# The mixers' output products of a decoder trunk: o stationary, 512 columns of weights moving, and turned back to features

## The chip, the cores and the metric

The kernel runs on one core of one Trainium2 chip. The time is that of the device in microseconds (us), the median of several runs. "Span" is the time from the first to the last instruction in one execution that the hardware profiler took.

## The reference

A trunk of two layers over 256 tokens of width 1024, in float32. Each layer is a half-weighted SwiGLU feed-forward (width 2816), a mixer with attention (16 heads of 64), and a second feed-forward; each has an RMSNorm ahead of it.

```python
for layer in range(DEPTH):
    h = h + 0.5 * swiglu(rmsnorm(h, ffn1_norm[layer]), ...)
    hn = rmsnorm(h, mix_norm[layer])
    h = h + (mixer_a(hn, ...) if layer == 0 else mixer_b(hn, ..., shared))
    h = h + 0.5 * swiglu(rmsnorm(h, ffn2_norm[layer]), ...)
    if layer == 0:
        shared = shared_kv(h, kv_norm, kv_w, pos)
return rmsnorm(h, final_norm)
```

Both mixers end in `o @ w_o`, where o is the attention's output (256 tokens by 1024) and w_o is 1024 by 1024. Mixer a takes q, k and v from one projection of the stream; mixer b takes q from its own norm of the stream and k, v from a second norm, the shared one. At this length mixer b's attention is plain causal attention, and mixer a's three dilated patterns become one mask with the logarithm of counts.

## The kernel before, in words

**Layout.** The stream is kept with features on the partitions: hT is 8 blocks of 128 features by 256 tokens. A norm (class Norm, L219) has three parts. `scale` (L231) writes a block of x = h times the gain, as a high part on ScalarE and a low part on VectorE (L98, L96); products are made as three, high by high, high by low, low by high, so that float32 is kept. `square` (L234) squares a block on ScalarE and adds it on GpSimd into ss (L237, L240, L241). `finish` (L243) lets TensorE sum ss over the partitions (L246: a column of one number for each token), VectorE add epsilon (L248: v_n) and GpSimd take the power -0.5 (L250: c_n). The norm's factor is applied after the product, at the evacuation.

**Weights** come in pieces: a DMA on the queue of SyncE into raw, ScalarE's copy wh (the high part), VectorE's difference wl (the low part). A piece of 128 by 1024 is one place of 8 in the pool wp; the class Pieces (L292) splits a few pieces ahead of their use. The feed-forward's first pieces (f20_g0, f20_u0, f20_g2 and so on, L166, L167) are split during the mixer's last part, some of them behind given instructions of the attention (`queued`, L145).

**Mixers** (L722) run products and attention interleaved on TensorE by a hand-written agenda (L266). The generator `projections` (L789) makes products of a segment of 512 columns of weights for two tiles of 128 tokens and says what each step of three matmuls costs (0.68). Calls due by the agenda's clock run in between: `norm.late` (the turning back that the feed-forward ahead has left over), `norm.finish` at 8.1 if the norm's column isn't there, and the attention's steps. `evacuate` (L767) takes a finished accumulator: ScalarE scales it by the column (rt, L772), VectorE rotates (L635 to L638), and `turn_in` (L752) is put on the agenda, which transposes q and k on TensorE (L761: qt) at 4.4 - 1.2t after the evacuation of the first segment. Then come scores (s), transposes of the weights of attention (pt, L682), their parts pT (L684, L687), products with v (po, L701, L703), and a block of the output, oT, with features on the partitions (L705, L710, L98, L94). There are 8 blocks; the last one also loads ScalarE's table for Silu (L718).

**Output products** (`out_t`, L591). For each block k of o, 4 accumulators of 2 blocks of output features by 256 tokens take 6 matmuls each: the weights are stationary (128 by 128) and o moves (256 columns). The pieces of the last three blocks are held until all of o is there; then each accumulator is finished in turn, VectorE adds it to hT (L622), the next norm scales the blocks, and after all of them the norm squares. The feed-forward (`ffn_blocks`, L351) follows, block k = 0 first, so it needs x of block 0 first.

**Down projections** (`down`, L542) already work the other way: tokens on the partitions, 512 columns of weights moving. Their results are turned back by 8 transposes for each pair of quarters (`turn`, L547 to L557), the second pair after the next stage has begun (`norm.late`).

Order: the Tile framework's scheduler sets each engine's order from the order of the program and its own estimates, so that an instruction's place in a queue can change when the program around it does.

Of the kernel before, what the change touches and what calls it, by code (L numbers as in the profile page):

```python
# [66 lines left out]
def trunk(ctx: ExitStack, tc: tile.TileContext, a: dict, out: bass.AP):  # L67
    nc = tc.nc
# [15 lines left out]
    def acc(name):  # L84
        return accp.tile([P, 512], F32, tag="acc", name=name)
# [18 lines left out]
    def trt(name):  # L104
        return trp.tile([P, 512], F32, tag="tr", name=name)
# [83 lines left out]
    def product(accs, xh, xl, ws, first, last):  # L189

        for ac, (wh, wl) in zip(accs, ws):
            nc.tensor.matmul(ac, xh, wh, start=first, stop=False)  # L192
        for ac, (wh, wl) in zip(accs, ws):
            nc.tensor.matmul(ac, xh, wl, start=False, stop=False)  # L194
        for ac, (wh, wl) in zip(accs, ws):
            nc.tensor.matmul(ac, xl, wh, start=False, stop=last)  # L196
# [252 lines left out]
    def quartered(name, w, acts, sums, weight, collected, tail=2):  # L449
# [89 lines left out]

        return close  # L540

    def down(name, w, acts, sums, norm):  # L542

        outs = []
        close = quartered(name, w, acts, sums, 0.5, outs.extend)

        def turn(c, half):  # L547
            tr = trt(f"dt_{name}_{c}_{half}")
            for i in range(2):
                for t in range(NT):  # L550
                    at = i * S + t * P
                    nc.tensor.transpose(tr[:, at:at + P], outs[t][c][:, (2 * half + i) * P:(2 * half + i + 1) * P], ident)
            d = 4 * c + 2 * half
            h = hT[:, d:d + 2, :]
            nc.vector.tensor_add(h, tr.rearrange("p (k s) -> p k s", s=S), h)
            for i in range(2):
                norm.block(d + i)  # L557

        def turn_first():
            for half in range(2):  # L560
                turn(0, half)

        for c in range(2):
            for t in range(NT):
                ac = close(t, c, between=turn_first if (t, c) == (0, 1) else None)
                nc.vector.scalar_tensor_tensor(outs[t][c], ac, 0.5, outs[t][c], op0=ALU.mult, op1=ALU.add)
        norm.late += [lambda half=half: turn(1, half) for half in range(2)]

    def down_last(name, w, acts, sums, h, weight, part, after):

# [20 lines left out]
    def out_t(name, pieces, base, blocks, norm, queue, tail=3):  # L591


        accs = [acc(f"ot_{name}_{i}") for i in range(KD // 2)]

        def step(i, k, ws):
            wh, wl = ws
            for j in range(2):
                d = slice((2 * i + j) * P, (2 * i + j + 1) * P)
                ac = accs[i][:, j * S:(j + 1) * S]  # L600
                hi, lo = blocks[k][:, 0, :], blocks[k][:, 1, :]
                nc.tensor.matmul(ac, wh[:, d], hi, start=k == 0 and j == 0, stop=False)
                nc.tensor.matmul(ac, wh[:, d], lo, start=False, stop=False)
                nc.tensor.matmul(ac, wl[:, d], hi, start=False, stop=k == KD - 1 and j == 1)

        for k in range(KD - tail):
            with queued(queue.get(k)):
                ws = pieces.get(base + k, 3)[0]
            while len(blocks) <= k:
                yield None  # L610
            for i in range(KD // 2):
                step(i, k, ws)
                yield 0.72
        held = [(k, pieces[base + k][0]) for k in range(KD - tail, KD)]
        while len(blocks) < KD:
            yield None
        for i in range(KD // 2):
            for k, ws in held:
                step(i, k, ws)
            for j in range(2):  # L620
                d = 2 * i + j
                nc.vector.tensor_add(hT[:, d, :], accs[i][:, j * S:(j + 1) * S], hT[:, d, :])  # L622
                norm.scale(d)
        for d in range(KD):
            norm.square(d)


    def rotate(v, t, name):
# [93 lines left out]
    def mixer(name, segs, plan, wo, mask, after, queue={}):  # L722

        n = HG * DH
        blocks, heads, qks, vss = [], {}, {}, {}
        specs = []
        for i, (norm, x, parts) in enumerate(segs):  # L730
            ends = [0]
            for part in parts:
                ends.append(ends[-1] + part[3])
            for k0 in range(0, KD, 4):
                specs.append((f"{''.join(part[0] for part in parts)}{name}{i}_{k0}", 4, ends[-1],
                              [(slice(at, at + c), rows(w, k0, 4, c0, c)) for at, (_, w, c0, c, _) in zip(ends, parts)]))
        base = 2 * len(specs)
        specs += [(f"{name}o_{u}", 2, D, [(None, rows(wo, 2 * u, 2, 0, D))]) for u in range(KD // 2)]
        pieces = Pieces(specs)
        agenda = Agenda()  # L740
        for norm in {id(norm): norm for norm, _, _ in segs}.values():
            for i in range(len(norm.late)):
                agenda.after(1.5 + 0.5 * i, lambda norm=norm: norm.late.pop(0)())
            if norm.col is None:
                agenda.after(8.1, norm.finish)
        scores, turn, values = attention(agenda, lambda g: (qks[g], vss.get(g)), mask, name, blocks)

        def turns(p):
            for i in range(2):
                turn(p, i)  # L750

        def turn_in(g, t):  # L752

            if t == 0:
                qks[g] = [ap_.tile([P, 4, NT, P], F32R, tag=f"qk{i}", name=f"qk{i}_{name}{g}", bufs=2) for i in "hl"]
            tr = trt(f"qt_{name}{g}_{t}")
            for i, kind in enumerate("qk"):
                s = heads[kind, g, t].rearrange("p a b -> p (a b)")
                for k in range(2):
                    at = (2 * i + k) * P  # L760
                    nc.tensor.transpose(tr[:, at:at + P], s[:, k * P:(k + 1) * P], ident)  # L761
            parts_of(*[x[:, :, t, :] for x in qks[g]], tr.rearrange("p (k n) -> p k n", n=P), later=agenda.soon)
            if t == NT - 1:
                for wait, step, p in plan[g]:
                    agenda.after(wait, {"s": scores, "t": turns, "v": values}[step], p)

        def evacuate(i, t, r, ac, parts):  # L767
            at, turned = 0, []
            wide = sum(c for kind, _, _, c, _ in parts if kind != "v")
            if wide:  # L770
                rt = atile([P, wide // DH, DH], name=f"rt_{name}{i}_{t}")
                nc.scalar.activation(flat(rt), ac[:, :wide], AF.Copy, scale=r)  # L772
# [12 lines left out]
            for g in sorted(set(turned)):  # L785
                if ("q", g, t) in heads and ("k", g, t) in heads:
                    agenda.after(4.4 - 1.2 * t if i == 0 else 3.2, turn_in, g, t)

        def projections():  # L789
            for i, (norm, x, parts) in enumerate(segs):  # L790
                acs = [acc(f"{''.join(part[0] for part in parts)}_{name}{i}_{t}") for t in range(NT)]
                for k0 in range(0, KD, 4):
                    for t in range(NT):
                        for k in range(k0, k0 + 4):
                            w = pieces[4 * i + k // 2][k % 2]
                            product([acs[t]], *x[t](k), [w], k == 0, k == KD - 1)
                            yield 0.68
                        if k0 + 4 == KD:
                            evacuate(i, t, norm.col[t], acs[t], parts)

        agenda.run(projections())
        agenda.run(out_t(f"{name}o", pieces, base, blocks, after, queue))
# [121 lines left out]
```

## Time and profile before

| | |
|---|---|
| median of 3 runs | 980.07 us (979.99 to 980.25) |
| the profiled execution | 980.13 us, span 978.4 |
| granted TensorE clock | 0.998 |
| mixer a, its output products | 277.8 to 307.8 us |
| mixer b, its output products | 758.2 to 789.35 us |
| TensorE busy in these two stretches | 29.73 of 30.00, 31.02 of 31.15 us |
| DMA over the span | 176.00 MB, 180 GB/s |

The page gives the busy time of each engine (PE is TensorE's matmuls, PEld its weight loads, DVE VectorE, ACT ScalarE, POOL GpSimd), and the chain of work that ended last. A row of the timeline has the start in us, the duration, the engine, the line, the operation, output<-inputs and the shape; idle time just before it stands in brackets, with what ended it. Matmuls overlap, so their cost is read from start to start. A row of the chain has the start, the time that the chain spent there, and what it was.

### The profile page before, as it was taken

Reading aid. Unit: us, or ns where it says so; the run is one execution under the profiler, and the core shown is the slowest. Engines: PE = TensorE matmul, PEld = TensorE weight load, DVE = VectorE, ACT = ScalarE, POOL = GpSimd, SP = SyncE. Lnnn points to the kernel's source line nnn. Section 1 sums busy time; section 2 is a strip of 40 time slices with the busy share of each in tenths; the row PEclk is TensorE's granted clock in tenths of the full one; section 3 lists DMA queues with packets and bytes.
Section 4 is the critical chain, followed back from the end, with each engine's and each line's share of the span. In section 5 each row is a group of like instructions: output and inputs, shape, how many; then the busy total and the mean of one; then the engine's idle time right before and its main releaser. Section 6 shows DMA issues by size and latency. Waiting matters only on the chain.

```text
span 978.4 us, 14860 instructions
## 1 busy us (share of the span) xinstructions
PE 967.5 (99%) x5391; PEld 831.9 (85%) x5391; DVE 813.0 (83%) x1383; ACT 612.7 (63%) x1131; POOL 287.0 (29%) x242
## 2 busy tenths in 40 slices
PE   8999999999999999999999999999999999999997
PEld 6888888878889888888888888888888998888886
DVE  7988899887878788889898888987787878888995
ACT  7655657567777665556576655655677756666561
POOL 3211246132332211146032121612142322112461
PEclk9999999999999999999999999999999999999999
DMA  9875536664334556546755556483734345564341
GB/s 317 259 238 187 197 133 216 219 212 157 133 98 152 180 186 189 184 153 208 256 172 173 172 177 212 169 277 114 249 131 136 116 145 172 186 202 173 130 172 43
DMA packets 126857, 176.00 MB, mean 180 GB/s; under 512 B 3392, under 2 KB 106304, under 8 KB 126784
## 3 DMA queue, kind: packets, MB, share of 16 engines
q1 hardware_dynamic: 125936, 174.01, 53.7%
q10 hardware_dynamic: 848, 1.05, 0.3%
q8 instruction: 42, 0.69, 0.3%
q14 instruction: 31, 0.25, 0.1%
HBM read 173.99 MB, written 1.05 MB: 179 GB/s over the span
## 4 chain that ended last, share of the span: by engine, by line
PE 92%; DVE 4%; ACT 2%; issue 1%; POOL 1%; DMA 0%; SPq 0%; POOLq 0%; DVEq 0%; ACTq 0%
PE f_g L203 16%; PE f_u L203 16%; PE f_u L206 8%; PE f_g L206 8%; PE dn_f_d L196 6%; PE dn_f_d L192 6%; PE dn_f_d L194 6%; PE dn_f_d_m L196 1%; PE dn_f_d_m L194 1%; PE dn_f_d_m L192 1%; PE qk_a L192 1%; PE qk_a L196 1%; PE qk_a L194 1%; DVE x_n L96 1%; PE q_b L192 1%
## 5 line engine op out<-in xcount | busy, mean ns | idle before, releaser
L368 POOL TENSOR_TENSOR j_f_u<-j_f_u,r_n 128x256 f32<-128x256 f32 x88 | 92.3, 1051 | 360.8 <-DVE j_f_u L336 338.0
L203 PE MATMUL f_g<-x_n,wh_f_g 128*128 128x512 f32 x688 | 180.5, 394 | 0.0
L203 PE MATMUL f_u<-x_n,wh_f_u 128*128 128x512 f32 x688 | 177.2, 390 | 0.0
L203 PEld LDWEIGHTS f_u<-x_n,wh_f_u 128*128 128x128 f32 x688 | 129.2, 188 | 27.3
L203 PEld LDWEIGHTS f_g<-x_n,wh_f_g 128*128 128x128 f32 x688 | 124.0, 189 | 22.7
L167 DVE TENSOR_TENSOR wl_f_u<-raw_f_u,wh_f_u 128x1024 fp32r<-128x1024 f32 x86 | 113.1, 1316 | 1.1 <-ACT wh_f_u L166 1.0
L167 DVE TENSOR_TENSOR wl_f_g<-raw_f_g,wh_f_g 128x1024 fp32r<-128x1024 f32 x86 | 104.3, 1230 | 2.8 <-ACT wh_f_g L166 2.8
L206 PE MATMUL f_u<-x_n,wl_f_u 128*128 128x256 f32 x688 | 103.3, 283 | 0.0
L206 PE MATMUL f_g<-x_n,wl_f_g 128*128 128x256 f32 x688 | 102.7, 282 | 0.0
L206 PEld LDWEIGHTS f_g<-x_n,wl_f_g 128*128 128x128 f32 x688 | 96.4, 190 | 6.3
L166 ACT ACTIVATE wh_f_u<-raw_f_u 128x1024 fp32r<-128x1024 f32 x86 | 88.0, 1049 | 12.0 <-PE f_g L203 7.5
L166 ACT ACTIVATE wh_f_g<-raw_f_g 128x1024 fp32r<-128x1024 f32 x86 | 89.6, 1049 | 4.7 <-PE f_g L203 2.8
L206 PEld LDWEIGHTS f_u<-x_n,wl_f_u 128*128 128x128 f32 x688 | 91.6, 192 | 0.0
L366 ACT ACTIVATE j_f_g<-j_f_g 128x256 f32<-128x256 f32 x88 | 36.7, 417 | 87.2 <-DVE j_f_g L365 86.9
L241 POOL TENSOR_TENSOR ss_n<-ss_n,sq_n 128x256 f32<-128x256 f32 x42 | 38.4, 913 | 148.8 <-ACT sq_n L240 146.8
L98 ACT ACTIVATE act_f<-j_f_g 128x256 fp32r<-128x256 f32 x58 | 23.9, 418 | 56.4 <-DVE j_f_g L376 56.4
L376 DVE TENSOR_TENSOR j_f_g<-j_f_g,j_f_u 128x256 f32<-128x256 f32 x58 | 27.9, 487 | 30.1 <-POOL j_f_u L368 30.1
L484 POOL TENSOR_TENSOR sum_f_d_6b<-sum_f_d_6ac,raw_f_d 128x512 f32<-128x512 f32 x4 | 45.5, 11371 | 17.6 <-DVE sum_f_d_6ac L483 13.2
L336 DVE TENSOR_TENSOR j_f_g<-f_g,j_f_g 128x256 f32<-128x256 f32 x88 | 36.6, 416 | 11.9 <-ACT j_f_g L335 11.9
L677 POOL TENSOR_SCALAR sm_b<-sm_b,ls_b 128x128 f32<-128x128 f32 (+1 forms) x32 | 28.5, 907 | 55.7 <-DVE ls_b L675 29.6
L335 ACT ACTIVATE j_f_u<-f_u 128x256 f32<-128x256 f32 x88 | 33.0, 375 | 15.0 <-PE row_n L258 14.0
L365 DVE TENSOR_TENSOR j_f_g<-j_f_g,r_n 128x256 f32<-128x256 f32 x88 | 41.4, 474 | 0.7
(565 smaller groups left out, 2369.3 us busy)
## 6 DMA issues: line engine op xcount, KB each, us to landing
raw_f_d<-in_ffn_w_down_dram SPq DMA_DIRECT2D x44, 1024.0 KB, 4.9
raw_f_g<-in_ffn_w_gate_dram SPq DMA_DIRECT2D x43, 1024.0 KB, 5.2
raw_f_u<-in_ffn_w_up_dram SPq DMA_DIRECT2D x43, 1024.0 KB, 5.2
raw_qka<-in_a_w_qkv_dram SPq DMA_DIRECT2D x16, 512.0 KB, 4.7
raw_va<-in_a_w_qkv_dram SPq DMA_DIRECT2D x4, 1024.0 KB, 5.4
raw_ao<-in_a_w_o_dram SPq DMA_DIRECT2D x4, 1024.0 KB, 4.9
raw_kvb<-in_kv_w_dram SPq DMA_DIRECT2D x8, 512.0 KB, 4.7
raw_qb<-in_b_w_q_dram SPq DMA_DIRECT2D x4, 1024.0 KB, 5.9
```

The source lines that it names most:

```text
L166: nc.scalar.activation(wh, r, AF.Copy)
L167: nc.vector.tensor_sub(wl, r, wh.bitcast(F32))
L192: nc.tensor.matmul(ac, xh, wh, start=first, stop=False)
L194: nc.tensor.matmul(ac, xh, wl, start=False, stop=False)
L196: nc.tensor.matmul(ac, xl, wh, start=False, stop=last)
L203: nc.tensor.matmul(ac, wh, flat(x), start=first and i == 0, stop=False)
L206: nc.tensor.matmul(ac[:, :S], wl, x[:, 0, :], start=False, stop=last and i == len(ws) - 1)
L241: nc.gpsimd.tensor_tensor(self.ss, self.ss, sq, op=ALU.add)
L365: nc.vector.tensor_mul(g, g, norm.row)
L366: nc.scalar.activation(g, g, AF.Silu)
L368: nc.gpsimd.tensor_tensor(u, u, norm.row, op=ALU.mult)
L484: nc.gpsimd.tensor_tensor(b[:, 0], ac[:, 0], raw[:, 3], op=ALU.add)
```

## The change

`out_t` now has the accumulators of a down projection: two tiles of tokens by two halves of 512 output features. A block of o is stationary (128 by 128 of it) and 512 columns of weights move, so that a block k takes 4 steps of three matmuls. At the end the quarters of the first half are finished for both token tiles, then those of the second half; ScalarE copies each quarter to SBUF, and the quarters are turned back to features by the function of the down projections, now shared (`turn_back`): the first half ahead of the last held block of quarter (0, 1), the second half by `norm.late` after the feed-forward's first block. The norm squares each block right behind its scaling.

In the mixers `norm.finish` is due at 8.7 for the first segment's norm and at 14.0 for another one (in mixer b: n5). An evacuation is put on the agenda rather than done at once, 0.6 later if the column isn't there yet. The second `turn_in` of the first segment is due 0.4 later.

```diff
     def out_t(name, pieces, base, blocks, norm, queue, tail=3):
-        accs = [acc(f"ot_{name}_{i}") for i in range(KD // 2)]
-        def step(i, k, ws):
-            wh, wl = ws
-            for j in range(2):
-                d = slice((2 * i + j) * P, (2 * i + j + 1) * P)
-                ac = accs[i][:, j * S:(j + 1) * S]
-                hi, lo = blocks[k][:, 0, :], blocks[k][:, 1, :]
-                nc.tensor.matmul(ac, wh[:, d], hi, start=k == 0 and j == 0, stop=False)
-                nc.tensor.matmul(ac, wh[:, d], lo, start=False, stop=False)
-                nc.tensor.matmul(ac, wl[:, d], hi, start=False, stop=k == KD - 1 and j == 1)
+        accs = [[acc(f"ot_{name}_{t}{c}") for c in range(2)] for t in range(NT)]
+        outs = [[None, None] for t in range(NT)]
+        def step(t, c, k, w):
+            x = tuple(blocks[k][:, i, t * P:(t + 1) * P] for i in range(2))
+            product([accs[t][c]], *x, [tuple(v[:, c * 512:(c + 1) * 512] for v in w)], k == 0, k == KD - 1)
...
-        for i in range(KD // 2):
-            for k, ws in held:
-                step(i, k, ws)
-            for j in range(2):
-                d = 2 * i + j
-                nc.vector.tensor_add(hT[:, d, :], accs[i][:, j * S:(j + 1) * S], hT[:, d, :])
-                norm.scale(d)
-        for d in range(KD):
-            norm.square(d)
+        for c in range(2):
+            for t in range(NT):
+                for k, w in held:
+                    step(t, c, k, w)
+                    if (t, c, k) == (0, 1, KD - 2):
+                        for half in range(2):
+                            turn_back(name, outs, 0, half, norm)
+                outs[t][c] = atile([P, 512], name=f"out_{name}_{t}{c}")
+                nc.scalar.activation(outs[t][c], accs[t][c], AF.Copy)
+        norm.late += [lambda half=half: turn_back(name, outs, 1, half, norm) for half in range(2)]
...
-                agenda.after(8.1, norm.finish)
+                agenda.after(8.7 if norm is segs[0][0] else 14.0, norm.finish)
...
-                    agenda.after(4.4 - 1.2 * t if i == 0 else 3.2, turn_in, g, t)
+                    agenda.after(4.4 - 0.8 * t if i == 0 else 3.2, turn_in, g, t)
...
-                            evacuate(i, t, norm.col[t], acs[t], parts)
+                            agenda.after(0.6 if norm.col is None else 0.0,
+                                         lambda t=t, i=i, norm=norm, ac=acs[t], parts=parts:
+                                         evacuate(i, t, norm.col[t], ac, parts))
```

More of the change, by code (lines that the diff above doesn't have):

```diff
@@ L540, in quartered, with turn_back @@
         return close
+    def turn_back(name, outs, c, half, norm):
+        tr = trt(f"dt_{name}_{c}_{half}")
+        for i in range(2):
+            for t in range(NT):
+                at = i * S + t * P
+                nc.tensor.transpose(tr[:, at:at + P], outs[t][c][:, (2 * half + i) * P:(2 * half + i + 1) * P], ident)
+        d = 4 * c + 2 * half
+        h = hT[:, d:d + 2, :]
+        nc.vector.tensor_add(h, tr.rearrange("p (k s) -> p k s", s=S), h)
+        for i in range(2):
+            norm.block(d + i)
     def down(name, w, acts, sums, norm):
@@ L545, in down @@
         close = quartered(name, w, acts, sums, 0.5, outs.extend)
[L547 to L557, printed above, removed]
         def turn_first():
             for half in range(2):
-                turn(0, half)
+                turn_back(name, outs, 0, half, norm)
         for c in range(2):
@@ L566, in down @@
                 nc.vector.scalar_tensor_tensor(outs[t][c], ac, 0.5, outs[t][c], op0=ALU.mult, op1=ALU.add)
-        norm.late += [lambda half=half: turn(1, half) for half in range(2)]
+        norm.late += [lambda half=half: turn_back(name, outs, 1, half, norm) for half in range(2)]
     def down_last(name, w, acts, sums, h, weight, part, after):
@@ L591, in out_t @@
     def out_t(name, pieces, base, blocks, norm, queue, tail=3):
-        accs = [acc(f"ot_{name}_{i}") for i in range(KD // 2)]
-        def step(i, k, ws):
-            wh, wl = ws
-            for j in range(2):
-                d = slice((2 * i + j) * P, (2 * i + j + 1) * P)
-                ac = accs[i][:, j * S:(j + 1) * S]
-                hi, lo = blocks[k][:, 0, :], blocks[k][:, 1, :]
-                nc.tensor.matmul(ac, wh[:, d], hi, start=k == 0 and j == 0, stop=False)
-                nc.tensor.matmul(ac, wh[:, d], lo, start=False, stop=False)
-                nc.tensor.matmul(ac, wl[:, d], hi, start=False, stop=k == KD - 1 and j == 1)
+        accs = [[acc(f"ot_{name}_{t}{c}") for c in range(2)] for t in range(NT)]
[3 more added lines that the diff above has]
+            product([accs[t][c]], *x, [tuple(v[:, c * 512:(c + 1) * 512] for v in w)], k == 0, k == KD - 1)
         for k in range(KD - tail):
             with queued(queue.get(k)):
-                ws = pieces.get(base + k, 3)[0]
+                w = pieces.get(base + k, 3)[0]
             while len(blocks) <= k:
                 yield None
-            for i in range(KD // 2):
-                step(i, k, ws)
-                yield 0.72
+            for t in range(NT):
+                for c in range(2):
+                    step(t, c, k, w)
+                    yield 0.68
         held = [(k, pieces[base + k][0]) for k in range(KD - tail, KD)]
@@ L616, in out_t @@
             yield None
-        for i in range(KD // 2):
-            for k, ws in held:
-                step(i, k, ws)
-            for j in range(2):
-                d = 2 * i + j
-                nc.vector.tensor_add(hT[:, d, :], accs[i][:, j * S:(j + 1) * S], hT[:, d, :])
-                norm.scale(d)
-        for d in range(KD):
-            norm.square(d)
+        for c in range(2):
+            for t in range(NT):
+                for k, w in held:
+                    step(t, c, k, w)
+                    if (t, c, k) == (0, 1, KD - 2):
+                        for half in range(2):
+                            turn_back(name, outs, 0, half, norm)
+                outs[t][c] = atile([P, 512], name=f"out_{name}_{t}{c}")
+                nc.scalar.activation(outs[t][c], accs[t][c], AF.Copy)
+        norm.late += [lambda half=half: turn_back(name, outs, 1, half, norm) for half in range(2)]
     def rotate(v, t, name):
```

## The prediction

> **What bounds the kernel now.** I read the page first: the busy shares, then the chain that ended last.
>
> ```profile
> PE 967.5 (99%) x5391; PEld 831.9 (85%) x5391; DVE 813.0 (83%) x1383; ACT 612.7 (63%) x1131; POOL 287.0 (29%) x242
> PE 92%; DVE 4%; ACT 2%; issue 1%; POOL 1%; DMA 0%; SPq 0%; POOLq 0%; DVEq 0%; ACTq 0%
> ```
>
> TensorE is busy nearly all the time and carries 92% of the chain. So two things count in the mixers: how long TensorE's own work takes there, start to start, and where it stands still. I went through the starts of its matmuls in the timeline and noted each place where the next one started late. An engine beside it counts only through such a place.
>
> **TensorE's work in the output products.** In the timeline of PE the steps from start to start are even.
>
> ```profile
> 299.17 0.28 PE L602 MATMUL ot_ao<-oT_a,wh_ao 128*128 128x256 f32 x1
> 307.81 0.40 PE L203 MATMUL f_g<-x_n,wh_f_g 128*128 128x512 f32 x1
> 187.51 0.39 PE L192 MATMUL dn_f_d<-wh_f_d_9a,act_f 128*128 128x512 f32 x1
> 190.23 0.39 PE L192 MATMUL qk_a<-wh_qka,x_n 128*128 128x512 f32 x1
> 185.94 0.27 PE L552 MATMUL dt_f_d<-ident,co_f_d_a 128*128 128x128 f32 x1
> 187.04 0.40 PE L194 MATMUL dn_f_d<-wl_f_d_10b,act_f 128*128 128x512 f32 x1
> ```
>
> The held tail of mixer a is 3 pieces x 4 accumulators x 6 = 72 matmuls of 256 columns, from 299.17 to 307.81: 0.120 us each. The 12 matmuls of 512 columns from 187.51 to 190.23 take 0.2267 each (the new form: activations stationary, weights moving). A mixer has 8 blocks; each costs 24 x 0.120 = 2.88 before and 12 x 0.2267 = 2.72 after. That is 23.04 against 21.76, **-1.28 per mixer, -2.56 in all**.
>
> The Trainium skill (TensorE: Matmul & The Clock Gate, Back-to-back issue gap) gives a warm matmul N/2.4 + 2.5 ns. An estimate from that page is 0.109 us for 256 columns and 0.216 for 512, which would save only 0.25 per mixer; the total below would be 2.06 higher. The rows above disagree with it in both forms (0.120 and 0.2267).
>
> The products now give tokens by features, so each mixer turns them back: two groups of 8 transposes. Such a group already stands in the down projections: 185.94 to 187.04 holds 8 transposes and one matmul of 512, so a group costs 1.10 - 0.23 = 0.87 to 0.88. Four new groups: **+3.52**. No engine hides this; TensorE itself does it. TensorE's work therefore grows by 0.96, and a gain can only come from its waits.
>
> **The start of mixer a** (the norm's column, L246). The column is moved one step of three matmuls back, the evacuation of the first product behind it.
>
> ```profile
> 195.55 4.43 POOL L241 TENSOR_TENSOR ss_n<-ss_n,sq_n 128x256 f32<-128x256 f32 x4 [3.85 <-ACT sq_n L240]
> 199.44 0.50 PE L196 MATMUL qk_a<-wh_qka,x_n 128*128 128x512 f32 x1
> 200.04 0.61 PE L246 MATMUL col_n<-mean,ss_n 128*128 128x1 f32 x4
> 200.50 0.48 PE L192 MATMUL qk_a<-wh_qka,x_n 128*128 128x512 f32 x1
> ...
> 800.66 0.50 PE L246 MATMUL col_n<-mean,ss_n 128*128 128x1 f32 x4
> 801.02 1.40 PE L203 MATMUL f_g<-x_n,wh_f_g 128*128 128x512 f32 x5
> ...
> 205.15 0.39 PE L196 MATMUL v_a<-wh_va,x_n 128*128 128x512 f32 x1
> 205.76 0.63 PE L761 MATMUL qt_a<-ident,rt_a 128*128 128x128 f32 x4 [0.23 <-ACT wh_qka L318]
> 207.38 0.40 PE L196 MATMUL v_a<-wh_va,x_n 128*128 128x512 f32 x1
> 207.95 0.63 PE L761 MATMUL qt_a<-ident,rt_a 128*128 128x128 f32 x4 [0.18 <-DVE rt_a L638]
> ```
>
> The sum on GpSimd ends at 199.98, TensorE was ready at 199.44 + 0.23 = 199.67, the column starts at 200.04: 0.37, and 0.10 more because 200.04 to 200.50 is 0.46 where an undisturbed column takes 0.36 (800.66 to 801.02). Moved back by 0.68 it starts at 200.35, after the sum: **-0.47**. But behind it TensorE waits twice more, 205.38 to 205.76 and 207.61 to 207.95, for the rotated tiles. What leads there is the chain of waits:
>
> ```profile
> 201.06 1.13 DVE wl_qka L320
> 202.20 0.08 DVE v_n L248
> ...
> 202.35 1.63 POOL c_n L250
> ...
> 204.01 0.04 ACT rt_a L772
> ```
> ```profile
> 204.73 0.29 DVE L635 TENSOR_TENSOR ra_a<-rt_a,rot 128x128 f32<-128x128 f32 x1 [1.33 <-ACT rt_a L772]
> 205.32 0.29 DVE L638 TENSOR_TENSOR rt_a<-ra_a,rb_a 128x128 f32<-128x128 f32 x1
> ```
>
> The column was ready at 200.65, yet v_n ran at 202.20: it stood in VectorE's queue behind weight splits. In the built order of the changed kernel one more split (the second half of qka2_0, 1.13) stands ahead of v_n. So v_n at 203.33, c_n until 205.1, rt_a at 205.15. VectorE's order also puts the second rt_a's first rotation (its evacuation starts 0.58 after the first) ahead of the last step of the first one. That step runs at about 206.65, and the transposes qt_a0_0 start 0.45 later, as 205.32 to 205.76 in before: 207.1. TensorE arrives at 200.35 + 0.45 + 9 x 0.2267 + 12 x 0.2267 = 205.55. It waits 1.55 in place of 0.38, **+1.17**. The second pair of transposes then finds its tile ready, **-0.34**. This place: +0.36. If v_n were not late, all three waits would go: -1.19. If the rotated tile were 0.3 later still, +0.66. I take the built order.
>
> **The middle of both mixers.** The evacuations come one product later, and everything that the agenda hangs on them moves along (the second turn_in, 4.4 - 0.8t, another 0.4); the distances from pt to po and from s to pt in the built order stay within three matmuls. One place had a wait:
>
> ```profile
> 290.03 0.28 PE L604 MATMUL ot_ao<-oT_a,wl_ao 128*128 128x256 f32 x1
> 290.43 0.88 PE L701 MATMUL po_a<-pT_a,vs_a 128*128 128x256 f32 x2
> 291.15 0.34 PE L703 MATMUL po_a<-pT_a,vs_a 128*128 128x128 f32 x2
> ```
>
> po_a6 was 0.28 late and took 0.72 where two matmuls of 256 take 0.24: 0.76 lost, waiting for pT's low part behind two weight splits on VectorE. Between pt_a6 and po_a6 stood 18 x 0.120 = 2.16 us of products; now 12 x 0.2267 = 2.72, and pt_a5, where VectorE's run of splits begins, has drawn a step away from po_a4. By my count the low part is ready within 0.1 of its use: **-0.76** (between 0 and that).
>
> **The start of mixer b.** Here the column of n5 waited for the same sum:
>
> ```profile
> 681.45 0.39 PE L196 MATMUL kv_b<-wh_kvb,x_kx 128*128 128x512 f32 x1
> 682.41 0.61 PE L246 MATMUL col_n<-mean,ss_n 128*128 128x1 f32 x4 [0.57 <-POOL ss_n L241]
> 682.87 0.48 PE L192 MATMUL kv_b<-wh_kvb,x_kx 128*128 128x512 f32 x1
> ```
>
> 681.68 to 682.41 is 0.73, and 0.10 again. It moves 5.9 on the agenda, into the second segment; the first segment uses n3's column, and c_n5 is first read by q's evacuation some 5 us later. **-0.83**, and nothing behind it.
>
> **The tails.** Once the last block of o is there, 9 matmuls run on held pieces per output quarter. In mixer b the built order puts them right behind po_b7, where before 6 small ones stood between, and VectorE splits g2_0 ahead of po_b7's sums, before it was behind.
>
> ```profile
> 781.65 0.28 PE L604 MATMUL ot_bo<-oT_b,wl_bo 128*128 128x256 f32 x1
> 781.98 0.50 PE L602 MATMUL ot_bo<-oT_b,wh_bo 128*128 128x256 f32 x2
> ...
> 780.57 0.85 DVE L710 TENSOR_TENSOR o_b<-po_b,o_b 64x256 f32<-64x256 f32 x2 [1.03 <-ACT o_b L705]
> 781.65 1.22 DVE L167 TENSOR_TENSOR wl_f_g<-raw_f_g,wh_f_g 128x1024 fp32r<-128x1024 f32 x1 [0.23 <-ACT wh_f_g L166]
> ...
> 781.52 0.40 ACT L98 ACTIVATE oT_b<-o_b 128x256 fp32r<-128x256 f32 x1
> ```
>
> Before, TensorE waited 0.21 here and lost a tenth in the next two. After, counted from the end of po_b7: VectorE is busy with u0_4 until 0.4, with block 6 until 0.7, with g2_0 until 1.85, with the sums until 2.65, ScalarE's high part is there at 3.1. TensorE has 11 x 0.2267 = 2.5 of work: 0.7 waited, **+0.39** net (bounds -0.31 and +1.2). In mixer a the two quarters of k = 4 still follow po_a7, and I count 0.
>
> New are the copies of the outputs on ScalarE (576 ns each) and the second turning back, one block into the feed-forward. Its model is the turning back ahead of mixer b:
>
> ```profile
> 668.30 0.27 PE L552 MATMUL dt_f_d<-ident,co_f_d_a 128*128 128x128 f32 x1
> ...
> 668.94 1.29 DVE L555 TENSOR_TENSOR gains_hT<-dt_f_d,gains_hT 128x512 f32<-128x512 f32 x2 [1.79 <-PE dt_f_d L552]
> ...
> 669.66 0.51 ACT L98 ACTIVATE x_n<-gains_hT 128x256 fp32r<-128x256 f32 x1 [7.59 <-DVE gains_hT L555]
> 672.51 3.89 ACT L318 ACTIVATE wh_qb<-raw_qb 128x1024 fp32r<-128x1024 f32 x4
> ...
> L504 ACT ACTIVATE co_f_d_a<-dn_f_d_m x4: 576/576/577, 169.4 to 951.9; 128x512 f32<-128x512 f32 x4
> ```
>
> ScalarE needs until 4.2 after the first transpose for four x and four squares (668.30 to 672.51). Then come both copies, done at 4.8 and 5.3. TensorE does the group, 12 matmuls and the first feed-forward block (8 matmuls, 1.39) and asks for the second copy at 5.2: 0.1 each, **+0.20** (0 to 1.2 if the copies come half a microsecond later each). The first turning back has 6 matmuls (1.36) to cover the copy of 0.6. The blocks x4 to x7, now squared in pairs with the scaling, are ready by 1.4 us or more, and the feed-forward's weight splits by over 4; the DMAs keep their order on the queue of SyncE.
>
> **Sum:** -2.56 + 3.52 + 0.36 - 0.76 - 0.83 + 0.39 + 0.20 = **+0.32**. The profiled execution took 980.13 (span 978.4): 980.45. The median of the runs is 0.06 under it, so I predict **980.4 us**.
>
> **Rivals.**
> - Covered: v_n comes early enough and all old waits go: -0.47 - 0.38 - 0.34 - 0.76 - 0.83 - 0.31 + 0.96 = -2.13, 977.9. For it: each of these waits is in the rows, and the column's move aims at three. Against it: VectorE's queue, not the sum, set v_n's time.
> - The last block is late in both tails (slower): the split of g2_0 needs the place of piece k = 4 and stands ahead of the last o. It decides once the high part comes more than 2.5 us after po_b7 (1.6 after the held products begin in mixer a). If it comes 1 us later than counted in each mixer: +2.0, 982.4. For it: VectorE runs without a gap there. Against it: the built order has pushed the products of block 7 behind those of block 6.
> - The new form saves nothing (it does not do what it is for): if a matmul of 512 costs here as much as two of 256, 2.56 is lost, 983.0. The skill's formula named above goes that way, with 982.5. Against it stand over a hundred matmuls of this form at 0.2267.
>
> **How the numbers follow.** A measurement of this kernel can tell about 0.2% (2 us) from no change. The forecast has 0.75, covered 0.09, the late block 0.13, the form 0.03. The range, 978.7 to 982.4, takes in the forecast with the bounds of its terms (all waits at once at their ends is unlikely) and touches the late block. Faster by over 0.2% needs nearly all of the covered case: 0.08. Slower by over 0.2% needs the late block or the form: 0.16. The rest, 0.76, lies within.
>
> **What would show it.** In the profile after: steps of 0.227 in the output products and groups of 8 transposes at 0.88; the column of n1 without a wait, v_n about 1.1 after its old place and a wait of 1 us or more ahead of the first qt_a; no wait at po_a6 and at the column of n5; a wait of 0.4 to 1.0 ahead of block 7 in mixer b's tail; hardly one at the second turning back. The prediction is wrong if v_n's place in the queue does not matter, or if new waits over 1 us stand at the turning back.

## The result, and the profile after

| | before | after |
|---|---|---|
| median of 21 runs each | 980.27 us (979.99 to 980.79) | 981.99 us (981.26 to 982.73) |
| the profiled execution | 980.13, span 978.4 | 981.9, span 980.1 |

The ratio is 1.0017, with a 95% interval of 1.0010 to 1.0023: 1.72 us slower, where +0.32 was forecast. The page after, its busy row and its chain:

```profile
PE 968.8 (99%) x5231; PEld 824.7 (84%) x5231; DVE 814.3 (83%) x1375; ACT 615.4 (63%) x1139; POOL 289.3 (30%) x242
PE 92%; DVE 4%; ACT 2%; issue 1%; DMA 0%; POOL 0%; SPq 0%; POOLq 0%; ACTq 0%; DVEq 0%
```

TensorE carries the same 92% of the chain, and its busy time grew by 1.3 (967.5 to 968.8). Where the time came in can be read from the starts of instructions that stand in both programs. First before, then after, in the timeline of PE:

```profile
277.77 0.28 PE L602 MATMUL ot_ao<-oT_a,wh_ao 128*128 128x256 f32 x1
...
319.12 0.50 PE L246 MATMUL col_n<-mean,ss_n 128*128 128x1 f32 x4
...
672.62 0.39 PE L192 MATMUL kv_b<-wh_kvb,x_kx 128*128 128x512 f32 x1
...
758.21 0.28 PE L602 MATMUL ot_bo<-oT_b,wh_bo 128*128 128x256 f32 x1
...
789.35 0.40 PE L203 MATMUL f_g<-x_n,wh_f_g 128*128 128x512 f32 x1
```
```profile
190.49 0.39 PE L192 MATMUL qk_a<-wh_qka,x_n 128*128 128x512 f32 x1
...
278.74 0.39 PE L192 MATMUL ot_ao<-wh_ao,oT_a 128*128 128x512 f32 x1
...
308.28 0.39 PE L203 MATMUL f_g<-x_n,wh_f_g 128*128 128x512 f32 x1
...
320.61 0.50 PE L246 MATMUL col_n<-mean,ss_n 128*128 128x1 f32 x4
...
674.06 0.39 PE L192 MATMUL kv_b<-wh_kvb,x_kx 128*128 128x512 f32 x1
...
758.74 0.50 PE L192 MATMUL ot_bo<-wh_bo,oT_b 128*128 128x512 f32 x1
...
790.28 0.39 PE L203 MATMUL f_g<-x_n,wh_f_g 128*128 128x512 f32 x1
...
802.42 0.50 PE L246 MATMUL col_n<-mean,ss_n 128*128 128x1 f32 x4
```

Differences after less before, in the order of the program: +0.26 at the first qk_a (190.49 against the prediction's 190.23; the code ahead of it is unchanged, and over the 14 profiles of this document that start lies anywhere from 190.10 to 191.00, so this part is scatter of single executions), +0.47 at f20's first product (308.28 against 307.81), +1.49 at the column behind it, +1.44 at mixer b's first product, +0.93 at f21's first, +1.76 at the last column (against 800.66). So mixer a with its first turning back cost 0.2, its second turning back 1.0; mixer b with its first turning back gained 0.5 and its second cost 0.8.

**Start of mixer a.** The timelines of PE, of DVE and of POOL after:

```profile
200.74 0.50 PE L246 MATMUL col_n<-mean,ss_n 128*128 128x1 f32 x4
201.10 0.49 PE L192 MATMUL qk_a<-wh_qka,x_n 128*128 128x512 f32 x1
...
205.78 0.39 PE L196 MATMUL v_a<-wh_va,x_n 128*128 128x512 f32 x1
207.35 0.63 PE L759 MATMUL qt_a<-ident,rt_a 128*128 128x128 f32 x4 [1.18 <-DVE rt_a L636]
...
209.88 0.60 PE L759 MATMUL qt_a<-ident,rt_a 128*128 128x128 f32 x4
```
```profile
201.25 2.35 DVE L320 TENSOR_TENSOR wl_qka<-raw_qka,wh_qka 128x1024 fp32r<-128x1024 f32 x2
203.53 0.15 DVE L248 TENSOR_SCALAR v_n<-col_n 128x2 f32<-128x2 f32 x1
```
```profile
203.75 1.62 POOL L250 TENSOR_TENSOR c_n<-v_n,expo 128x2 f32<-128x2 f32 x1 [3.50 <-DVE v_n L248]
```

The column takes its undisturbed 0.36 and doesn't wait (-0.46). v_n, whose column was done at 201.24, ran at 203.53 behind two splits of weights; the first qt, which TensorE asked for at 206.01 (one step of 0.23 after 205.78), started at 207.35. Its wait of 1.34 stands in place of 0.38 (+0.96); the second qt has none (-0.37).

**A wait that the prediction did not have**, at the first po of mixer a; PE after, DVE after, then DVE before:

```profile
227.56 0.28 PE L699 MATMUL po_a<-pT_a,vs_a 128*128 128x256 f32 x1
228.06 0.39 PE L699 MATMUL po_a<-pT_a,vs_a 128*128 128x256 f32 x1 [0.23 <-DVE pT_a L685]
```
```profile
225.07 2.47 DVE L320 TENSOR_TENSOR wl_qka<-raw_qka,wh_qka 128x1024 fp32r<-128x1024 f32 x2 [0.78 <-ACT wh_qka L318]
227.46 1.01 DVE L685 TENSOR_TENSOR pT_a<-pt_a,pT_a 128x384 fp32r<-128x384 f32 x2
```
```profile
223.62 1.22 DVE L320 TENSOR_TENSOR wl_qka<-raw_qka,wh_qka 128x1024 fp32r<-128x1024 f32 x1 [1.00 <-ACT wh_qka L318]
224.76 1.01 DVE L687 TENSOR_TENSOR pT_a<-pt_a,pT_a 128x384 fp32r<-128x384 f32 x2
225.69 1.21 DVE L320 TENSOR_TENSOR wl_qka<-raw_qka,wh_qka 128x1024 fp32r<-128x1024 f32 x1
```

The second matmul of po_a0 started 0.50 after the first where 0.12 is usual, and with its after-effects the place lost 0.50: pT's low part ran behind two splits in a row. Before, VectorE made one split, then pT, then the other split.

**Output products and turning back**, PE after:

```profile
292.17 0.64 PE L699 MATMUL po_a<-pT_a,vs_a 128*128 128x256 f32 x2
292.65 0.33 PE L701 MATMUL po_a<-pT_a,vs_a 128*128 128x128 f32 x2
...
293.89 0.47 PE L192 MATMUL ot_ao<-wh_ao,oT_a 128*128 128x512 f32 x1
294.20 0.39 PE L194 MATMUL ot_ao<-wl_ao,oT_a 128*128 128x512 f32 x1
...
296.05 0.39 PE L192 MATMUL ot_ao<-wh_ao,oT_a 128*128 128x512 f32 x1
...
304.68 1.04 PE L548 MATMUL dt_ao<-ident,out_ao 128*128 128x128 f32 x8
305.47 0.48 PE L192 MATMUL ot_ao<-wh_ao,oT_a 128*128 128x512 f32 x1
305.79 0.39 PE L194 MATMUL ot_ao<-wl_ao,oT_a 128*128 128x512 f32 x1
...
308.06 0.39 PE L196 MATMUL ot_ao<-wh_ao,oT_a 128*128 128x512 f32 x1
...
309.69 1.19 PE L548 MATMUL dt_ao<-ident,out_ao 128*128 128x128 f32 x8
310.63 0.48 PE L203 MATMUL f_g<-x_n,wh_f_g 128*128 128x512 f32 x1
```

From 305.79 to 308.06 ten steps take 0.227 each. Behind short matmuls the first step is 0.31 (293.89 to 294.20, behind pt; 0.32 from 305.47 to 305.79, behind a turning back). The next eight take 0.231 on average behind this pt (294.20 to 296.05), but 0.227 behind the turning back. A first turning back takes 304.68 to 305.47 and 0.09 more in the next step: 0.89, with mixer b's the same. The second ones take 1.03 (309.69 to 310.63, and 0.09 more) and, in mixer b, 1.02 by the same count. po_a6 still lost 0.24 (292.17 to 292.65 where two matmuls take 0.24).

**Mixer b**, PE after: the column of n5 is in the second segment and takes 0.36; in the tail, block 7's high part was late.

```profile
689.28 0.50 PE L246 MATMUL col_n<-mean,ss_n 128*128 128x1 f32 x4
689.64 0.47 PE L192 MATMUL q_b<-wh_qb,x_n 128*128 128x512 f32 x1
...
782.75 0.39 PE L194 MATMUL ot_bo<-wl_bo,oT_b 128*128 128x512 f32 x1
783.59 0.50 PE L192 MATMUL ot_bo<-wh_bo,oT_b 128*128 128x512 f32 x1 [0.44 <-ACT oT_b L98]
783.92 0.40 PE L194 MATMUL ot_bo<-wl_bo,oT_b 128*128 128x512 f32 x1
```

782.75 to 783.59 is 0.61 more than a step, and 0.10 follows: 0.71 against 0.41 before.

### The profile page after: what moved, and what is told of

Read it like the earlier page. It is cut to its first block, busy times and chain, and to the rows that moved or that the text cites. A ratio compares the mean times of both kernels' runs of the same rounds, so it can differ in the third digit from the quotient of the medians.

```text
span 980.1 us, 14536 instructions
## 1 busy us (share of the span) xinstructions
PE 968.8 (99%) x5231; PEld 824.7 (84%) x5231; DVE 814.3 (83%) x1375; ACT 615.4 (63%) x1139; POOL 289.3 (30%) x242
## 4 chain that ended last, share of the span: by engine, by line
PE 92%; DVE 4%; ACT 2%; issue 1%; DMA 0%; POOL 0%; SPq 0%; POOLq 0%; ACTq 0%; DVEq 0%
PE f_g L203 16%; PE f_u L203 16%; PE f_u L206 8%; PE f_g L206 8%; PE dn_f_d L194 6%; PE dn_f_d L196 6%; PE dn_f_d L192 6%; PE dn_f_d_m L194 1%; PE dn_f_d_m L196 1%; PE dn_f_d_m L192 1%; PE qk_a L192 1%; PE qk_a L196 1%; PE qk_a L194 1%; PE q_b L192 1%; PE ot_ao L192 1%
## 5 line engine op out<-in xcount | busy, mean ns | idle before, releaser
L675 POOL TENSOR_SCALAR sm_a<-sm_a,ls_a 128x128 f32<-128x128 f32 (+1 forms) x32 | 30.1, 956 | 47.3 <-DVE ls_a L673 41.3
```

What stands on the lines that cost most here:

```text
L675: nc.gpsimd.tensor_scalar(sm[:, seg], sm[:, seg], ls[:, t:t + 1], None, op0=ALU.mult)
```

## The experiments

**Theory.** The result is a sum of parts that hardly touch each other: the new products save less than their turning back costs; mixer a's new schedule costs about 1 us, through VectorE's queue (v_n, and pT at po_a0); n5's column gains 0.8. **Rivals:** the schedule as a whole is a gain and only the products cost; or the products cost nothing and the schedule is all of it; or the waits have another cause than VectorE's queue. All times below are medians of 11 runs (9 for the last) beside the median of the kernel before that was measured with them (980.37, 980.44 and 980.43); an interval of a ratio is about 0.0009 to either side, 0.9 us. So differences of half a microsecond rest on the traces, not on the medians alone. Between the first qk_a, the first ot_ao, f20's first product, the first ot_bo and f21's first product all these kernels run the same matmuls (but for the output products and their transposes), so that the lengths of these stages can be compared from trace to trace.

### The parts apart

Only the products (constants and the direct evacuation of before):

```diff
-                agenda.after(8.7 if norm is segs[0][0] else 14.0, norm.finish)
+                agenda.after(8.1, norm.finish)
-                    agenda.after(4.4 - 0.8 * t if i == 0 else 3.2, turn_in, g, t)
+                    agenda.after(4.4 - 1.2 * t if i == 0 else 3.2, turn_in, g, t)
-                            agenda.after(0.6 if norm.col is None else 0.0, lambda ...)
+                            evacuate(i, t, norm.col[t], acs[t], parts)
```

> The changed kernel with the norm's column, the evacuation and the turning in of the heads scheduled as before; only the output products and their turning back are new. Theory (read from the profile after): the products save 0.95 us per mixer, not 1.28, the four groups cost 0.89, 1.03, 0.89, 1.03, po_a6 gives back 0.5 and the tails cost 0.4: -1.90 + 3.84 - 0.5 + 0.4 = +1.84 over the kernel before, about 982.1 us. Rival (the working on record, with nothing lost in the products): -2.56 + 3.52 - 0.76 + 0.39 + 0.20 = +0.79, about 981.1. If the schedule is what costs, it stays within 0.5 of the kernel before.

981.67, +1.30 (ratio 1.0013, 1.0004 to 1.0022). The new products cost time by themselves; the sum on record for this part (+0.79) and the reading of the trace (+1.84) lie on either side of it. Its trace has the first qt waiting as before.

Only the schedule: the three edits of the changed kernel, in the kernel before.

> The kernel before with only the new schedule (column of n1 one step later, of n5 at 14.0, the evacuation behind the column, the second turning in 0.4 later); the output products are the old ones. Theory: column n1 -0.46, first qt +0.96, second qt -0.37, po_a0 +0.50, column n5 -0.83: -0.2 against the kernel before, about 980.1. Rival (the schedule is what the record missed): +0.9 or more. The record: 0.36 - 0.83 = -0.47, and po_a6 keeps its 0.76.

981.25, +0.88 (1.0009, 1.0000 to 1.0018). My number missed by 1.1, and the rival's came. Mixer a behaves as in the changed kernel: from the first qk_a to the first ot_ao it takes 88.26 where it was 87.55 before, 0.71 more (in the changed kernel 88.25), and -0.46 + 0.96 - 0.37 + 0.50 is 0.63. The column of n5 gains its 0.8 too. But mixer b hands it back in the output stage, in the timeline of PE:

```profile
763.13 0.49 PE L682 MATMUL pt_b<-ident,sm_b 128*128 128x128 f32 x3
763.96 0.52 PE L682 MATMUL pt_b<-ident,sm_b 128*128 128x128 f32 x3 [0.33 <-DVE nm_b L664]
...
782.75 0.28 PE L604 MATMUL ot_bo<-oT_b,wl_bo 128*128 128x256 f32 x1
783.45 0.50 PE L602 MATMUL ot_bo<-oT_b,wh_bo 128*128 128x256 f32 x2 [0.41 <-ACT oT_b L98]
```

The second half of pt_b4 comes 0.50 late, and block 7 of the tail 0.69 after its forerunner, 0.36 more than the 0.33 of before: 0.86 in all. By the stages, mixer b's output products take 32.10 here, 31.15 before. So the delayed evacuations (each one product later) cost mixer b something too, which I had put at nothing; old_form_mended below, with the same schedule but direct evacuations in mixer b, takes 31.19 there. Beside the new products this loss hardly shows: 31.54 in the changed kernel against 31.44 in products_n5 below, which has the direct evacuations. So the parts do not simply add up: the new products cost only 0.84 on top of this run (1.72 - 0.88), less than the 1.30 that they cost alone.

Only the column of n5, in the kernel before:

```diff
-                agenda.after(8.1, norm.finish)
+                agenda.after(8.1 if norm is segs[0][0] else 14.0, norm.finish)
```

> The kernel before with one edit: the column of n5 comes at 14.0 on mixer b's agenda, that of n1 stays at 8.1. Theory: the wait of 0.73 and its 0.10 go and nothing takes their place: -0.83, about 979.4. Rival: the wait returns behind it, at the next place that waits for VectorE: within 0.2 of the kernel before.

979.61, -0.76 (0.9994, 0.9985 to 1.0003). In its trace mixer b loses nothing behind it. The wait is gone, as the theory has it.

The changed kernel with n5's column at 14.0 and the rest of the schedule as before:

> The changed kernel with mixer a's schedule as before (column of n1 at 8.1, evacuation right behind the product, turning in at 4.4 - 1.2t); the column of n5 stays at 14.0. Theory: the run products_only less 0.83: about 981.3, so 0.6 under the changed kernel, v_n in its old place, the first qt waiting 0.38 and po_a0 without its new 0.50. Rival: mixer a's schedule gains as a whole, and this is 0.5 or more over the changed kernel.

980.82, +0.45 (1.0006, 0.9998 to 1.0015). Against products_only that is -0.85 for n5; against the changed kernel, -1.27 for mixer a's schedule and the evacuations. Of this the traces place 0.80 ahead of the first ot_ao (88.25 against 87.45) and 0.19 in mixer a's output products (29.54 against 29.35). By the two pairs the products cost +1.30 and 0.45 + 0.76 = +1.21, so they add up with n5 as independent parts.

### What sets the first turning in

One instruction of the changed kernel is put on another engine; the order of TensorE's work stays the same.

```diff
-            nc.vector.tensor_scalar_add(v, ps[:, :NT], EPS)
+            nc.scalar.activation(v, ps[:, :NT], AF.Copy, bias=EPS) if self.name == "n1" else nc.vector.tensor_scalar_add(v, ps[:, :NT], EPS)
```

> The changed kernel with one instruction moved: v_n of the norm n1 runs on ScalarE instead of VectorE, so it no longer stands behind the weight splits; the order of TensorE's work is the same. Theory (VectorE's queue sets the first turning in): v_n at about 201 instead of 203.5, c_n done by 202.9, the first qt ready at about 205 where TensorE asks at 206.0: its wait of 1.35 goes and po_a0's 0.50 stays, so 1.2 to 1.4 under the changed kernel, about 980.7 us. Rival (the wait has another end, such as GpSimd's power or ScalarE's rt_a): less than 0.4 is gained, about 981.7.

980.63, +0.19 (1.0000, 0.9992 to 1.0009): 1.5 less than the changed kernel's +1.72. Timelines of ACT, POOL and PE of this run:

```profile
200.88 0.17 ACT L248 ACTIVATE v_n<-col_n 128x2 f32<-128x2 f32 x1 [1.58 <-PE col_n L246]
```
```profile
201.13 1.50 POOL L250 TENSOR_TENSOR c_n<-v_n,expo 128x2 f32<-128x2 f32 x1 [1.28 <-ACT v_n L248]
```
```profile
205.57 0.60 PE L759 MATMUL qt_a<-ident,rt_a 128*128 128x128 f32 x4
...
208.09 0.60 PE L759 MATMUL qt_a<-ident,rt_a 128*128 128x128 f32 x4
```

v_n runs 2.65 earlier, c_n too (0.39 of it because the opening of this execution was shorter: the first qk_a starts at 190.10, in the changed kernel at 190.49), and both qt stand without idle time ahead of them. From the first qk_a to the first ot_ao it takes 86.84, 1.41 less. The whole wait came from v_n's place in VectorE's queue. In the same trace po_a0 is still late (0.52 from its first matmul to its second), so that is another wait.

The first po of mixer a, one product later:

```diff
-          [steps(0, 3.0, 8.0, 11.0, 13.8, 16.5, 19.3), steps(1, 3.0, 8.0, 11.0, 13.8, 16.5, 19.3), steps(2, 4.0, 9.2),
+          [steps(0, 3.0, 8.0, 11.0, 14.5, 16.5, 19.3), steps(1, 3.0, 8.0, 11.0, 13.8, 16.5, 19.3), steps(2, 4.0, 9.2),
```

> The changed kernel with the first po of mixer a one product (0.7) later in the plan: 14.5 instead of 13.8. Theory: po_a0 came before pT's low part, which stands behind two weight splits; one product of three matmuls covers 0.68, so the 0.50 goes: about 981.5. Rival: the late block only moves the wait to the next po: no difference, 982.0.

981.42, +0.98 (1.0011, 1.0002 to 1.0020): 0.7 less than the changed kernel. The trace shows po_a0 without its gap (0.23 to the next row, as in an undisturbed po), and 0.5 gained at all later places.

```profile
228.46 0.40 PE L699 MATMUL po_a<-pT_a,vs_a 128*128 128x256 f32 x2
228.69 0.34 PE L701 MATMUL po_a<-pT_a,vs_a 128*128 128x128 f32 x2
```

### What the turning back costs

This kernel leaves the transposes out, so what it returns is not the trunk's output.

```diff
-        tr = trt(f"dt_{name}_{c}_{half}")
-        for i in range(2):
+        tr = outs[half][c] if name.endswith("o") else trt(f"dt_{name}_{c}_{half}")
+        for i in range(0 if name.endswith("o") else 2):
```

> The changed kernel without the transposes behind the output products (32 in all): the sums add the token-major outputs as they are, so the result is another one; the adds, copies and all else stay. Theory: the four groups cost what their matmuls take on TensorE, 0.89 + 1.03 + 0.89 + 1.03 = 3.84, and cover nothing: about 978.2, so the new products with their schedule are 2.1 under the kernel before. Rival: the groups partly cover ScalarE's copies and the next blocks x, and waits of 0.5 or more come up in their place: 978.9 or more.

978.18, -2.26 (0.9977, 0.9969 to 0.9986): 4.0 less than the changed kernel, where 3.84 was expected. f20's first product starts at 307.32, 0.96 ahead of the changed kernel's 308.28, and the second group takes another 1.0 with it. The transposes lie wholly on TensorE's path and cover nothing else.

```profile
307.32 0.39 PE L203 MATMUL f_g<-x_n,wh_f_g 128*128 128x512 f32 x1
```

### Both forms with the waits taken away

The kernel before with n5's column at 14.0 and v_n of n1 on ScalarE (both edits above):

> The kernel before with the column of n5 at 14.0 and v_n of n1 on ScalarE; the old output products. Theory: the waits of 0.38 and 0.34 ahead of both first qt go beside n5's 0.76: 1.5 under the kernel before, about 978.9. Rival: the second wait stays, since its rt_a stands behind a weight split on both engines: about 979.2.

978.79, -1.65 (0.9984, 0.9975 to 0.9992). Both first qt have no idle time ahead of them.

The changed kernel with v_n on ScalarE and the later first po:

> The changed kernel with both repairs of its schedule: v_n of n1 on ScalarE and the first po of mixer a at 14.5. Theory: both waits go, 1.35 + 0.5 under the changed kernel, about 980.1: as fast as the kernel before, because the new products with their turning back cost what the schedule gains. Rival (one repair spoils the other, VectorE's queue is reordered again): 980.6 or more.

980.00, -0.43 (0.9994, 0.9985 to 1.0003). Both waits go together, 2.1 under the changed kernel.

The old products with the same schedule; only the evacuation that has no column yet is put off:

```diff
-                            evacuate(i, t, norm.col[t], acs[t], parts)
+                            close = lambda t=t, i=i, norm=norm, ac=acs[t], parts=parts: evacuate(i, t, norm.col[t], ac, parts)
+                            agenda.after(0.6, close) if norm.col is None else close()
```

> The old output products with the whole of that schedule: column of n1 one step later with its first evacuation behind it, v_n on ScalarE, first po of mixer a at 14.5, column of n5 at 14.0; the other evacuations as before. Theory: the run with n5 and v_n alone less the column's 0.46: about 978.3, and 1.8 under the changed kernel with both repairs, which is the price of the new products alone. Rival: the column's gain is lost again at the first po: 978.8.

978.54, -1.89 (0.9980, 0.9972 to 0.9989). It gains less over n5_vn_act than the column's 0.46, but no wait came back at the first po. Against `mended` the old products are 1.46 faster: the price of the new form where the schedule's waits are out of the way, close to the 1.21 and 1.30 above. (The two differ also in the evacuations of mixer b.)

A later po_a6, in n5_vn_act and in old_form_mended:

```diff
-        return [(at + 2.6 * i + wait, step, 4 + i) for i in range(4) for wait, step in ((0.0, "t"), (2.3, "v"))]
+        return [(at + 2.6 * i + wait, step, 4 + i) for i in range(4) for wait, step in ((0.0, "t"), (3.0 if (i, at) == (2, 8.4) else 2.3, "v"))]
```

> The kernel before with n5 at 14.0, v_n of n1 on ScalarE and po_a6 one step of products (0.7) later. Theory: po_a6 comes behind pT's low part, its 0.76 becomes 0.0 to 0.2: about 978.2. Rival: the block of po_a6 is then late for the tail of mixer a, or the wait only moves: 978.8.

978.30, -2.13 (0.9978, 0.9969 to 0.9987).

> The old output products, the whole repaired schedule and po_a6 one step later: column n1, first and second qt, po_a6 and column n5 all without their waits. Theory: 2.5 under the kernel before, about 977.8, the fastest of all. Rival: 978.3, as without the last edit.

978.06, -2.37 (0.9976, 0.9966 to 0.9985): the lowest median of all kernels here, 4.1 under the changed one by these differences. The last edit brought 0.5 in both kernels, where 0.6 and 0.7 were expected by theory; that is less than the intervals, but mixer a's output products take 0.39 and 0.38 less in the traces (29.65 in both). The trace shows why it can't bring all of po_a6's 0.76. po_a6 is late no more, but po_a7 now is, by 0.32:

```profile
293.73 0.28 PE L604 MATMUL ot_ao<-oT_a,wl_ao 128*128 128x256 f32 x1
294.17 0.47 PE L701 MATMUL po_a<-pT_a,vs_a 128*128 128x256 f32 x2 [0.15 <-DVE o_a L710]
```

## Why the prediction was off by 1.4 us, step by step

The time on record, 980.4, was 1.6 too low. Of this 0.2 is the kernel before, whose median of 21 runs is 980.27 and not 980.07; the change itself was put at +0.32 and measured +1.72.

| step | on record | in the profile after |
|---|---|---|
| products | -2.56 | about -1.8 |
| turning back, with its second waits | +3.72 | +3.83 |
| column of n1 | -0.47 | -0.46 |
| first qt | +1.17 | +0.96 |
| second qt | -0.34 | -0.37 |
| po_a0 | 0 | +0.50 |
| po_a6 | -0.76 | -0.52 |
| column of n5 | -0.83 | -0.83 |
| tails | +0.39 | about +0.4 |
| sum | +0.32 | about +1.7 |

- **The products were mis-sized.** From the first ot_ao to f20's first product it is 30.04 before and 29.54 after, with a turning back of 0.89 in it: -1.39, of which po_a6 is -0.52 and a small wait in the tail +0.13, so about -1.0 for the products, not -1.28. In mixer b it is 31.14 and 31.54: -0.49 without the turning back, tail +0.30, about -0.8. I had taken 0.2267 from a run of products that nothing interrupts. In the mixers' output stage half of the steps come within eight of an interruption and take 0.230, and the first one 0.31 (before: 0.20 in place of 0.12, about as much). That names some 0.25 per mixer. That the interruption itself makes the eight steps slower is not shown: behind the turning back they take 0.227, and the same place can have 0.228 in one run and 0.231 in another. In mixer b the first steps differ too: they take 0.31 on average after, 0.19 before, so that each of the eight loses 0.02 more than before, another 0.16; under 0.1 stays open. The runs put the whole of the new form (products, turning back, po_a6, tails) at 1.2 to 1.5, the rows of the changed kernel at about 1.9, the record at 0.8. The lengths of the stages close most of that gap. Mixer a's output products with their first turning back take 29.35 in products_only and products_n5, not 29.54, and mixer b's 31.43 and 31.44, not 31.54: 0.3 of what the table books on the products and the tails comes only with the new schedule, mixer a's wait of 0.13 among it. The rest, up to 0.2 us for each second turning back, is the scatter of the last item.
- **The turning back was right**: groups of 0.89 on TensorE's path, nothing beside them. no_turning measured 4.0 for all four. The second ones were 0.13 dearer, where 0.10 was counted for the wait for the second copy; no run tests that it is this wait.
- **v_n's place was right**, in kind and size: it ran one split later (1.07 once the opening's 0.26 is taken off; the split was put at 1.13). The wait was 1.34 instead of 1.55, because TensorE came 0.2 later than counted. vn_act shows the cause. The case "covered" (977.9) is what n5_vn_act and old_form_mended come near to, and only with the old products.
- **"The distances from pt to po and from s to pt in the built order stay within three matmuls"** is the step that failed in mixer a. The distance on TensorE did stay (12 matmuls between pt and po, before and after); what changed was VectorE's order at po_a0: two splits ahead of pT's low part instead of one. I had looked for this at v_n and at the tails, and not at each po. It cost 0.50, and po_late takes it away.
- **po_a6** gave back two thirds of its 0.76; the low part came 0.24 late, not within 0.1.
- **The column of n5 and the tail of mixer b** were right: -0.83, and +0.30 for +0.39; n5_only measured -0.76 and products_n5 0.85 by difference. That nothing stands behind n5's column holds where the evacuations are direct; in schedule_only, with the old products, mixer b's put-off evacuations lost as much again (0.86).
- **The rivals.** The last block was late by 0.13 in mixer a and by 0.6 in mixer b, not by 1 us more than counted in each, so that 982.4 came out near the result by luck. The new form did save something (1.8 of the 2.56), so the third rival is wrong. The formula of the Trainium skill (TensorE: Matmul & The Clock Gate, Back-to-back issue gap), which that page gives for an isolated matmul, makes a step of 512 columns 0.216 us by estimate. Here it is 0.227 undisturbed and 0.230 in the mixers. The total that I had worked out from it (982.5) lies 0.5 from the measured time: a near sum from wrong terms.
- The rest of the profile's difference of 1.77 is +0.26 in the opening stage, which is scatter (above), and about -0.2 in f21's first blocks. There 26 pairs of a 512-column and a 256-column step take 0.346 each, where the same 26 pairs of f20 in the same execution, and of the kernel before, take 0.354; in products_n5 both feed-forwards have the faster pairs, in products_only both the slower. So it goes with the execution; the cause stays open.

## What to carry to other kernels

Moving a small instruction "behind the sum it waits for" gains little if the next link of its chain then stands behind long work in another engine's queue (here 0.46 gained, 0.96 lost): follow the whole chain (column, v_n, c_n, rt, qt) through each engine's queue, and move the one link that stands behind long work; here one instruction on another engine was worth 1.5 us. A cheaper form of a matmul has to pay for the layout that it leaves behind, at full price where TensorE is the bound: about 1.8 us saved against 3.8 us of transposes. And after each edit of an order compare VectorE's queue at every consumer on TensorE, not just at the places that waited before.

## What the runs showed of the hardware that I had not expected

- A step of 512 columns (float32, three-part products) is 0.227 us in a long run, but 0.31 right behind transposes, after which it is 0.227 to 0.231 at once; steps of 256 columns are 0.20 once and then 0.12. So a form's price depends a little on how often it is interrupted.
- The power on GpSimd (c_n, two numbers per partition) took 0.70 to 0.72 us in 54 of the 84 places where these 14 traces have it; no VectorE instruction was under way there at its start. In the other 30 it ended 0.56 to 0.58 after the VectorE instruction that was running when it started: 1.49 to 1.63 behind a weight split that had just begun (after: c_n from 203.75 to 205.37, the split from 203.59 to 204.80), 0.71 where the split was nearly done, 0.87 or 0.88 behind a shorter instruction. When n5's column moved to a place without a split, its c_n went from 1.61 (before) to 0.70 (after). It looks as if c_n waited for that instruction, but no run tests this alone. So in mixer a's first turning in, splits of weights delayed c_n as well as v_n; in vn_act c_n still took 1.50.
